# Sixty-four of 512 tokens leave the dense expert products and take gathered rows instead

## The chip, the core and the metric

The kernel runs on one core of a Trainium2 chip. A core has five engines that run their own instruction queues and meet at semaphores: PE (matrix products; its weight loads are listed apart as PEld), DVE (vector work), ACT (activations and copies), POOL (general work, and the queue of the software-made DMAs) and SP (which here only issues DMAs). SBUF is the on-chip memory of 128 partitions, PSUM the banks that PE writes. The metric is the device time of one execution in microseconds. The kernel before takes 2653.66 us, the median of three runs (2651.48 to 2654.41).

## The reference, cut to what matters

512 tokens of width 1024 go through two blocks. The first has a mixer (stick-breaking attention and a gated linear recurrence side by side) and then a PEER feed-forward; the second has a sliding-window layer and a sparse-attention layer. The change touches the mixer and the PEER part:

```python
def rg_lru(x, w_a, b_a, w_x, b_x, lam):       # x has been through a short causal convolution
    r = sigmoid(block_product(x, w_a) + b_a)
    i_gate = sigmoid(block_product(x, w_x) + b_x)
    log_a = -8.0 * r * softplus(-lam)
    b = sqrt(-expm1(2.0 * log_a)) * (i_gate * x)
    h_t = exp(log_a)_t * h_{t-1} + b_t        # a scan over the 512 tokens
o_rg = rg_lru(...) * gelu(g_rg)               # the gate multiplies what the scan gives

def peer_ffn(x, w_query, sub_keys, expert_u, expert_v):
    # 8 heads; each picks 16 of 16384 experts by two halves of a key
    idx, best_s = top16 of the sums of two top16 lists
    g = softmax(best_s)
    u = expert_u[idx]; v = expert_v[idx]      # one row of 1024 each
    act = gelu(x . u)
    return sum over the 128 picks of g * act * v
```

So a token needs 128 rows of U and 128 rows of V. All arithmetic is held to float32: a product is made of two rounded halves, hi and lo, and three matmuls (hi hi, hi lo, lo hi).

## The kernel before, in words

Activations lie transposed, features on the partitions and the 512 tokens along the row. Weights come as units of 512 KB. `Stream` loads a unit on SP's queue (`_dma`), rounds it to hi on ACT (`_hi`, line 145) and makes lo on DVE (`_lo`, line 154; on POOL for the units listed in `ON_POOL`). `gemm` (line 319) multiplies a unit: eight k-steps of three matmuls.

**The PEER part does not gather.** It computes the products of all 16384 experts with all tokens, in 128 chunks of 128 experts, and multiplies them by a dense matrix of gates that is zero for what a token did not pick. It has two stages:

- The s stage, 128 turns of `s_gemm` (line 937): 24 matmuls of 512 columns (lines 944 to 946), gelu on ACT, and a store to Sd in DRAM. Beside it runs the side work, `topk` (line 1047), as a Python generator whose steps `pace` mixes between the matmuls. A step yields its assumed cost on DVE and ACT, and `RATE` says how much of each fits into a chunk. Per tile of 128 tokens it finds the picks (`topk_tile`), and then in 32 steps of four tokens (`gate_tile`) builds the dense gates out of one-hot rows: comparisons on DVE, scaled copies on ACT, four or eight small products on PE, and stores to Gd in DRAM. The side work has to be over at chunk 122, where its memory is handed to the y stage.
- The y stage, 32 groups of four chunks. `w_part` (line 961) multiplies a chunk's s and gates (loaded back two chunks ahead by `prefetch` on POOL's queue) and splits the result: W on DVE, Wh on ACT, Wl on DVE. `y_part` (line 977) does 12 matmuls for one eighth of the features over the four chunks and adds them to the residual X on DVE. Each chunk of a group is followed by two `y_part`s.

**The mixer's order is written out by hand.** A projection takes eight slots, one per k-step. `put(i, f)` hangs a piece of other work on a slot, `take` hands the next eight to the unit that is being multiplied, and `self.at` is the first slot not yet taken. Every piece is thus issued behind a known matmul, on whatever engine it uses. The projections run: k and q of the first head pair, four g units (the gates, with the pieces of the bias table hung on them), four x units (each followed by convolution and two small gate products), four v units, and the next k and q. The recurrence's pieces (`rg_a` to `rg_e`, lines 638 to 655 and 527 to 535) hang on the slots after the x units, beside the v, k and q projections.

Of the kernel before, what the change touches and what calls it, by code (L numbers as in the profile page):

```python
# [42 lines left out]
TAIL = 6  # L43
WARM = 3

RATE = (4.6, 4.4)
# [67 lines left out]
ON_POOL = {"m": (1, 13, 15, 17, 26), "s": (2,), "n": (17,)}  # L114
# [93 lines left out]
class K:  # L208
# [267 lines left out]
    def mixer(self, dp, out_pool, bias):  # L476
# [50 lines left out]
        def rg_d(ct):  # L527
            s, u = xc[:, ct], it[:, ct]
            nc.vector.tensor_tensor_scan(s, rt[:, ct], u, 0.0, op0=MUL, op1=ADD)
            nc.gpsimd.tensor_tensor(u, gs[:, ct], s, op=MUL)  # L530

        def rg_e(ct):
            u = it[:, ct]
            square(ssr, u, ct == 0)
            self.gain_split(rgh[:, ct], rgl[:, ct], u, self.v("out_norm_rg", ct))


        with self.pool("maux", bufs=4, space=PSUM) as aux:
# [48 lines left out]
            def gelu(cs):  # L587
# [3 lines left out]
                nc.scalar.preload_act_table_set("sigmoid_and_others")  # L591
# [31 lines left out]

            for ct in range(4):
# [24 lines left out]
            def rg_c(ct):  # L649
                nc.vector.scalar_tensor_tensor(xc[:, ct], xc[:, ct], 2.0, y[ct], op0=MUL, op1=MUL)  # L650
                nc.gpsimd.tensor_tensor(it[:, ct], it[:, ct], xc[:, ct], op=MUL)
# [204 lines left out]
    def peer_pre(self, hraw, H):  # L856
# [5 lines left out]
        sgp = self.tc.alloc_tile_pool(name="sgp", bufs=2)  # L862
        tk = self.tc.alloc_tile_pool(name="tk", bufs=1)
        rscol = tk.tile([P, 4], F32, name="rscolf")
        top = lambda t: (tk.tile([P, 16, 16], F32, tag=f"tv{t % 2}", name="tv"),
                     tk.tile([P, 16, 16], U32, tag=f"ti{t % 2}", name="ti"), set())
        self.top = {t: top(t) for t in range(2)}
# [55 lines left out]
    def peer_main(self, sgp, tk, sc, rscol, H, Gd, Sd, pools, sums, fin):  # L923


        nc = self.nc
# [10 lines left out]
        def s_gemm(c, side=None):  # L937
            w = self.S.get(self.ui)
            self.ui += 1
            ps = sp.tile([P, T], F32, tag="s", name="s")  # L940
            hi, lo = w
            for k in range(KT):
                wh, wl = hi[:, k * P:(k + 1) * P], lo[:, k * P:(k + 1) * P]
                nc.tensor.matmul(ps, wh, h_hi[:, k], start=k == 0, stop=False)  # L944
                nc.tensor.matmul(ps, wh, h_lo[:, k], start=False, stop=False)  # L945
                nc.tensor.matmul(ps, wl, h_hi[:, k], start=False, stop=k == KT - 1)  # L946
# [4 lines left out]
        def prefetch(c):  # L951
            if c >= NCH:
                return
            g = pp.tile([P, T], F32, tag="G", name="G")
            nc.gpsimd.dma_start(g, Gd[c])  # L955
            s = pp.tile([P, T], F32, tag="sg", name="sg")
# [4 lines left out]
        def w_part(c):  # L961
# [7 lines left out]
            w = pp.tile([P, T], F32, tag="W", bufs=2, name="W")  # L969
            wh = pp.tile([P, T], F32R, tag="Wh", bufs=8, name="Wh")  # L970
            wl = pp.tile([P, T], F32R, tag="Wl", bufs=8, name="Wl")
# [5 lines left out]
        def y_part(gr, m):  # L977
            ps = yp.tile([P, T], F32, tag="y", name="y")
# [8 lines left out]
            nc.vector.tensor_tensor(self.X[:, m], self.X[:, m], ps, op=ADD)  # L987
            if gr == NG - 1:
                fin(m)

        side = self.topk(tk, gtp, gbp, ggp, trp, sc, rscol, Gd)
        cost = [0.0, 0.0]
        nside = NPRE - TAIL
# [13 lines left out]
        for c in range(NPRE):  # L1007
            if c == nside:
# [11 lines left out]
                yp = self.tc.alloc_tile_pool(name="pm_y", bufs=4, space=PSUM)  # L1020
            if c == NPRE - 5:
# [4 lines left out]
            ps = s_gemm(c, pace(c) if c < nside else None)  # L1026
            sg = sgp.tile([P, T], F32, tag="sg", name="sgo")
            nc.scalar.activation(sg, ps, AF.Gelu_apprx_tanh)  # L1028
            nc.gpsimd.dma_start(Sd[c], sg)  # L1029
            if c >= NPRE - 4:  # L1030
                w_part(c - (NPRE - 4))
        for gr in range(NG):
            self.S.vmax = 4 * (gr + 2)
            for j in range(4):
# [3 lines left out]
                y_part(gr, 2 * j + 1)  # L1038
# [1163 lines left out]
```

## Time and profile before

| | us |
|---|---|
| median of three runs | 2653.66 (2651.48 to 2654.41) |
| the profiled execution's own time | 2653.56 |
| its span, first to last instruction | 2651.7 |
| mixer | 0 to 262 |
| queries, scores and the start of top-k | 262 to 378.7 |
| s stage | 378.7 to 1188.7 |
| y stage | 1188.7 to 1909.5 |
| the two attention layers of the second block | 1909.5 to 2651.7 |

The ends of the stages are the first starts of the lines that belong to them. Over the span PE is busy 97%, DVE 69%, ACT 54% and POOL 16%. The granted TensorE clock is 0.991 of full speed. Matmuls are pipelined, so that the 0.4 us the profile gives for one of 512 columns is its length, and not the distance to the next one; distances are read from starts.

In the views below, a group's row has line, engine, operation, output and inputs by name, sizes and count, then the busy time in us and the mean length of one in ns, then the engine's idle time before it and what ended it. A timeline row has start and length in us. A row of waits has who waited for whom, the total in us, how often, and the longest. Where a matmul is in full float32 (not split into halves), the trace has two records for it.

### The profile page before, as it was taken

The page shows a single profiled execution, that of the slowest core. Times are in us where ns is not written, and L with a number is a line of the kernel's source. Part 1 is how long each engine was busy: PE and PEld are TensorE (multiplying, and loading weights), DVE is VectorE, ACT ScalarE, POOL GpSimd, SP SyncE. Part 2 cuts the span into 40 slices and gives each one's busy share as a digit, 9 for nine tenths or more (in the row PEclk, how much of TensorE's full clock was granted, in tenths as well). Part 3 has the DMA queues.
Part 4 walks back from the last instruction along what each step waited for, and adds up shares of the span by engine and source line. Part 5 has one row for each costly group of instructions (what it writes and reads, how often), then busy time and mean ns, then how long its engine had stood idle before and what let it go on. Part 6 is the DMA issues. An engine that isn't in the chain of part 4 may idle for free.

```text
span 2651.7 us, 33669 instructions
## 1 busy us (share of the span) xinstructions
PE 2584.7 (97%) x11920; PEld 2043.9 (77%) x11920; DVE 1829.8 (69%) x3674; ACT 1418.8 (54%) x2822; POOL 420.4 (16%) x615
## 2 busy tenths in 40 slices
PE   8889999999999999999999999999999989999998
PEld 5667778888888878788888888888777777777776
DVE  5787668777868869536666666666578634777774
ACT  5585434887787788532222222222377534656653
POOL 3313001011011100021111111111211120101011
PEclk9999999999999999999999999999999999999999
DMA  4221224377477676756555555555232252212113
GB/s 150 64 64 56 96 96 157 130 198 202 144 193 204 174 191 182 212 203 203 190 191 190 187 187 190 188 186 185 85 93 77 70 159 84 88 62 65 62 61 103
DMA packets 230936, 372.65 MB, mean 141 GB/s; under 512 B 147583, under 2 KB 147711, under 8 KB 230640
## 3 DMA queue, kind: packets, MB, share of 16 engines
q1 hardware_dynamic: 56016, 201.88, 22.9%
q0 software_dynamic: 40928, 131.74, 16.2%
q10 hardware_dynamic: 133824, 36.89, 6.4%
q8 instruction: 94, 1.54, 0.2%
q14 instruction: 74, 0.61, 0.1%
HBM read 293.76 MB, written 79.82 MB: 141 GB/s over the span
## 4 chain that ended last, share of the span: by engine, by line
PE 84%; DVE 8%; ACT 3%; issue 2%; DMA 1%; ACTq 1%; POOL 1%; SPq 0%; DVEq 0%; POOLq 0%
PE y L986 9%; PE y L985 9%; PE y L984 9%; PE s L944 9%; PE s L946 9%; PE s L945 9%; PE g L326 6%; PE g L328 6%; PE g L327 6%; PE gps L1214 2%; PE nO L1849 1%; PE gps L1207 1%; PE hp L1605 1%; PE nL L1792 1%; PE nT L1831 1%
## 5 line engine op out<-in xcount | busy, mean ns | idle before, releaser
L154 DVE TENSOR_TENSOR lo<-raw,hi 128x1024 fp32r<-128x1024 f32 x374 | 456.8, 1229 | 191.4 <-PE s L946 94.0
L145 ACT ACTIVATE hi<-raw 128x1024 fp32r<-128x1024 f32 x381 | 395.0, 1052 | 94.2 <-PE y L985 38.8
L944 PE MATMUL s<-h_hi,hi 128*128 128x512 f32 x1024 | 409.2, 400 | 3.8 <-ACT hi L145 2.3
L946 PE MATMUL s<-h_hi,lo 128*128 128x512 f32 x1024 | 406.6, 397 | 0.5 <-DVE lo L154 0.5
L986 PE MATMUL y<-Wh,lo 128*128 128x512 f32 x1024 | 405.9, 396 | 0.0
L985 PE MATMUL y<-Wl,hi 128*128 128x512 f32 x1024 | 405.9, 396 | 0.0
L984 PE MATMUL y<-Wh,hi 128*128 128x512 f32 x1024 | 405.9, 396 | 0.0
L945 PE MATMUL s<-h_lo,hi 128*128 128x512 f32 x1024 | 403.6, 394 | 0.0
L973 ACT ACTIVATE Wh<-W 128x512 fp32r<-128x512 f32 x128 | 80.9, 632 | 418.5 <-DVE W L972 418.5
L1195 ACT ACTIVATE ohg<-oh,gh 128x128 fp32r<-128x128 bf16 x960 | 292.6, 395 | 5.3 <-DVE oh L1177 5.3
L987 DVE TENSOR_TENSOR X<-X,y 128x512 f32<-128x512 f32 x256 | 175.1, 685 | 149.0 <-PE y L986 147.0
L946 PEld LDWEIGHTS s<-h_hi,lo 128*128 128x128 f32 x1024 | 192.9, 188 | 48.5 <-DVE lo L154 1.3
L985 PEld LDWEIGHTS y<-Wl,hi 128*128 128x128 f32 x1024 | 192.9, 188 | 47.1
L984 PEld LDWEIGHTS y<-Wh,hi 128*128 128x128 f32 x1024 | 192.9, 188 | 47.0
L986 PEld LDWEIGHTS y<-Wh,lo 128*128 128x128 f32 x1024 | 192.9, 188 | 47.0
L944 PEld LDWEIGHTS s<-h_hi,hi 128*128 128x128 f32 x1024 | 193.5, 189 | 43.6 <-ACT hi L145 2.7
L945 PEld LDWEIGHTS s<-h_lo,hi 128*128 128x128 f32 x1024 | 193.2, 189 | 41.7
L1029 POOL DMA_DIRECT2D Sd<-sgo x128 | 69.6, 544 | 820.2 <-ACT sgo L1028 820.2
L1028 ACT ACTIVATE sgo<-s 128x512 f32<-128x512 f32 x128 | 76.3, 596 | 219.3 <-issue 137.8
L1177 DVE TENSOR_TENSOR oh<-cst,sT 128x512 bf16<-128x512 f32 (+1 forms) x256 | 164.9, 685 | 24.7 <-ACT ohg L1195 24.1
L974 DVE TENSOR_TENSOR Wl<-W,Wh 128x512 fp32r<-128x512 f32 x128 | 88.6, 692 | 105.8 <-ACT Wh L973 105.8
L955 POOL DMA_DIRECT2D G<-Gd x128 | 68.7, 537 | 542.4 <-DVE W L972 542.2
(457 smaller groups left out, 4765.1 us busy)
## 6 DMA issues: line engine op xcount, KB each, us to landing
raw<-in_peer_u_dram SPq DMA_DIRECT2D x128, 512.0 KB, 3.8
raw<-in_peer_v_dram SPq DMA_DIRECT2D x128, 512.0 KB, 3.3
Sd<-sgo POOLq DMA_DIRECT2D x128, 256.0 KB, 3.2
Gd<-Gb ACTq DMA_DIRECT2D x64, 512.0 KB, 4.7
G<-Gd POOLq DMA_DIRECT2D x128, 256.0 KB, 4.1
sg<-Sd POOLq DMA_DIRECT2D x128, 256.0 KB, 4.2
raw<-in_b_w_in_dram SPq DMA_DIRECT2D x33, 512.0 KB, 3.2
raw<-in_w_in_dram SPq DMA_DIRECT2D x20, 512.0 KB, 3.3
```

Source lines behind the costliest of these rows:

```text
L145: self.k.nc.scalar.activation(hi, self.r[i], AF.Copy)
L154: eng.tensor_tensor(lo, raw, hi.bitcast(F32), op=SUB)
L326: nc.tensor.matmul(ps, wh, rh[:, k - k0], start=start and k == k0, stop=False)
L944: nc.tensor.matmul(ps, wh, h_hi[:, k], start=k == 0, stop=False)
L945: nc.tensor.matmul(ps, wh, h_lo[:, k], start=False, stop=False)
L946: nc.tensor.matmul(ps, wl, h_hi[:, k], start=False, stop=k == KT - 1)
L984: nc.tensor.matmul(ps, vh, wh, start=j == 0, stop=False)
L985: nc.tensor.matmul(ps, vh, wl, start=False, stop=False)
L986: nc.tensor.matmul(ps, vl, wh, start=False, stop=j == 3)
L987: nc.vector.tensor_tensor(self.X[:, m], self.X[:, m], ps, op=ADD)
L1177: nc.vector.tensor_tensor(o, iota[:, None, :].to_broadcast([P, 4, P]), sT[:, x, 4 * q:4 * q + 4][:, :, None].to_broadcast([P, 4, P]), op=EQ)
L1195: nc.scalar.activation(B[q][:, j, x], oh[:, j], AF.Copy, scale=gh[:, x, 4 * q + j:4 * q + j + 1])
```

## The change

The last 64 tokens (`NGT`) leave the dense scheme; `TD` = 448 remain. Five things are edited.

1. **Dense products.** In both stages the matmuls, the gelu, W, Wh, Wl, the X additions, and the Sd and Gd rows go over 448 columns.
2. **Gates.** `gate_tile` runs 16 of its 32 steps for the last token tile. Two instructions keep that tile's picks: `pick_i`, the expert's number, and `pick_g`, its gate, both with the 128 picks on the partitions and the 64 tokens along the row.
3. **Gathered rows.** A second generator, `gather`, runs beside the y stage. It first turns the 64 tokens' h back to tokens on partitions (16 small products, two copies). Per token it gathers 128 rows of U (512 KB) by an indirect DMA on POOL's queue, spreads the token's h over all partitions with a matmul against a repeated column of an identity, and on DVE multiplies and sums (`scalar_tensor_tensor` with `accum_out`, two halves of 512). After 64 tokens come gelu and gates, and then per pair of tokens four products of the gathered V rows with a 32-column weight that is zero but for one column, so that each token's result adds up in its own row of one PSUM bank, `acc`. The rows use the buffers that held the split U units (five of 512 KB), and are asked for three ahead. The generator is advanced after each chunk of the y stage, and once more in every second group.
4. **Pacing.** `RATE` goes from (4.6, 4.4) to (4.2, 4.0), and the memory is handed over as soon as the side work is done, if that is before chunk 122.
5. **Mixer.** The x units come before the g units. The g units now run behind the first three parts of the recurrence, and its scan and what follows hang on the slots after them. Four kinds of elementwise work of the recurrence and three lo splits go from POOL to DVE. The activation tables are reloaded in another order.

```diff
-RATE = (4.6, 4.4)
+NGT = 64
+TD = T - NGT
+RATE = (4.2, 4.0)
-ON_POOL = {"m": (1, 13, 15, 17, 26), "s": (2,), "n": (17,)}
+ON_POOL = {"m": (1, 26), "s": (2,), "n": (17,)}
...
         def rg_d(ct):
             s, u = xc[:, ct], it[:, ct]
             nc.vector.tensor_tensor_scan(s, rt[:, ct], u, 0.0, op0=MUL, op1=ADD)
-            nc.gpsimd.tensor_tensor(u, gs[:, ct], s, op=MUL)
+            nc.vector.tensor_tensor(u, gs[:, ct], s, op=MUL)
         def rg_e(ct):
-            square(ssr, u, ct == 0)
+            square(ssr, u, ct == 0, eng=nc.vector)
...
-            for ct in range(4):
-                self.peq = self.take()
-                ps = self.unit(gp, xh, xl)
-                self.put(self.at, gate_in, ct, ps)
-                if bias:
-                    self.put(self.at + 0, bias.pop(0))
-            self.put(self.at + 2, gelu, range(4))
...
-                    nc.gpsimd.tensor_tensor(it[:, ct], it[:, ct], xc[:, ct], op=MUL)
+                    nc.vector.tensor_tensor(it[:, ct], it[:, ct], xc[:, ct], op=MUL)
...
-                for j, g in ((3, rg_a), (6, rg_b), (9, rg_c), (10, rg_d), (16, rg_e)):
-                    self.put(i0 + 6 + 6 * ct + j, g, ct)
+                for j, g in ((3, rg_a), (6, rg_b), (9, rg_c)):
+                    self.put(i0 + 6 + 5 * ct + j, g, ct)
+            for ct in range(4):
+                self.peq = self.take()
+                ps = self.unit(gp, xh, xl)
+                self.put(self.at, gate_in, ct, ps)
+                if bias:
+                    self.put(self.at + 0, bias.pop(0))
+            self.put(self.at + 2, gelu, range(4))
+            for ct in range(4):
+                self.put(self.at + 7 + 4 * ct, rg_d, ct)
+                self.put(self.at + 20 + 8 * ct, rg_e, ct)
...
+                xh, xl = h_hi[:, k, 0:TD], h_lo[:, k, 0:TD]
+                nc.tensor.matmul(ps, wh, xh, start=k == 0, stop=False)
...
+        def gather():
+            hT = gq.tile([P, D], F32R, tag="hT", name="hT")
+            id2 = gq.tile([P, NGT], F32R, name="id2")
+            nc.vector.tensor_tensor(id2, ident[:, 0:NGT], ident[:, NGT:P], op=ADD)
+            for half in range(2):
+                ps = yp.tile([P, T], F32, tag="y", name="hTp")
+                for k in range(4):
+                    for x, hh in enumerate((h_hi, h_lo)):
+                        nc.tensor.matmul(ps[x * NGT:(x + 1) * NGT, k * P:(k + 1) * P],
+                                         hh[:, 4 * half + k, TD:].bitcast(F32), ident, start=k == 0,
+                                         stop=True, skip_group_check=True)
+                nc.scalar.activation(hT[:, half * T:(half + 1) * T], ps, AF.Copy)
+            order = [(0, t) for t in range(NGT)] + [(1, 32 * p + j) for j in range(32)
+                                                    for p in range(2)]
+            def fetch(i):
+                if i < len(order):
+                    x, t = order[i]
+                    x5 = i % 5 % 2
+                    rows[i] = wp.tile([P, D], F32, tag=("hi", "lo")[x5], bufs=3 - x5, name="row")
+                    nc.gpsimd.indirect_dma_start(
+                        rows[i], None, tables[x],
+                        bass.IndirectOffsetOnAxis(ap=idx[:, t:t + 1], axis=0))
+            yield
+            for i in range(3):
+                fetch(i)
+            yield
+            for t in range(NGT):
+                r = rows.pop(t)
+                for half in range(2):
+                    o = slice(half * T, (half + 1) * T)
+                    bc = sp.tile([P, T], F32, tag="s", name="hrow")
+                    nc.tensor.matmul(bc, id2[:, t:t + 1].to_broadcast([P, P]), hT[:, o],
+                                     start=True, stop=True)
+                    nc.vector.scalar_tensor_tensor(r[:, o], r[:, o], 1.0, bc, op0=MUL, op1=MUL,
+                                                   accum_out=dots[:, half, t:t + 1])
+                fetch(t + 3)
+                yield
+            w = gq.tile([P, NGT], F32, name="gw")
+            nc.vector.tensor_tensor(w, dots[:, 0], dots[:, 1], op=ADD)
+            nc.scalar.activation(w, w, AF.Gelu_apprx_tanh)
+            nc.vector.tensor_tensor(w, w, gate, op=MUL)
+            acc = yap.tile([P, T], F32, name="yacc")
+            for j in range(32):
+                yield
+                r = [rows.pop(NGT + 2 * j + p) for p in range(2)]
+                wx = gq.tile([P, 2, 32], F32, tag="wx", bufs=3, name="wx")
+                for p in range(2):
+                    nc.vector.tensor_scalar(wx[:, p], iota[:, 0:32], float(j),
+                                            w[:, 32 * p + j:32 * p + j + 1], op0=EQ, op1=MUL)
+                for half in range(2):
+                    for p in range(2):
+                        q = 32 * (2 * p + half)
+                        nc.tensor.matmul(acc[q:q + 32, :], wx[:, p],
+                                         r[p][:, half * T:(half + 1) * T], start=j == 0,
+                                         stop=j == 31, skip_group_check=True)
+                fetch(NGT + 2 * j + 3)
+                fetch(NGT + 2 * j + 4)
+                yield
...
+            if c == NPRE - 2:
+                next(rest)
         for gr in range(NG):
+            if gr == NG - 2:
+                for _ in rest:
+                    pass
+            if gr % 2 == 1:
+                next(rest, None)
             for j in range(4):
                 if gr + 1 < NG:
                     w_part(4 * (gr + 1) + j)
                 y_part(gr, 2 * j)
                 y_part(gr, 2 * j + 1)
+                next(rest, None)
...
+        nq = 16 if tt == 3 else 32
-        for q in range(35):
+        for q in range(nq + 3):
...
-        first = [("k", 0), ("q", 0)] + [(t, i) for t in "gxv" for i in range(4)] + [("k", 1), ("q", 1)]
+        first = [("k", 0), ("q", 0)] + [(t, i) for t in "xgv" for i in range(4)] + [("k", 1), ("q", 1)]
```

At the end of `gather`, `acc` is copied, turned by four transposes and added to the last 64 tokens of X in two instructions. The rows of U come from a second copy of the table that lies by expert (`peer_ur`); V already does.

More of the change, by code (lines that the diff above doesn't have):

```diff
@@ L866, in peer_pre @@
                      tk.tile([P, 16, 16], U32, tag=f"ti{t % 2}", name="ti"), set())
+        self.picked = (tk0.tile([P, NGT], U32, name="pick_i"), tk0.tile([P, NGT], F32, name="pick_g"))
         self.top = {t: top(t) for t in range(2)}
@@ L939, in s_gemm @@
             self.ui += 1
-            ps = sp.tile([P, T], F32, tag="s", name="s")
+            ps = sp.tile([P, T], F32, tag="s", name="s")[:, 0:TD]
             hi, lo = w
@@ L977, in y_part @@
         def y_part(gr, m):
-            ps = yp.tile([P, T], F32, tag="y", name="y")
+            ps = yp.tile([P, T], F32, tag="y", name="y")[:, 0:TD]
             for j in range(4):
@@ L986, in y_part @@
                 nc.tensor.matmul(ps, vl, wh, start=False, stop=j == 3)
-            nc.vector.tensor_tensor(self.X[:, m], self.X[:, m], ps, op=ADD)
+            nc.vector.tensor_tensor(self.X[:, m, 0:TD], self.X[:, m, 0:TD], ps, op=ADD)
             if gr == NG - 1:
                 fin(m)
+        tables = A["peer_ur"], A["peer_v"].rearrange("c p d -> (c p) d")
+        idx, gate = self.picked
+        wp = pools["w"]
+        def gather():
+            ident, iota = self.c("ident"), self.c("iota")
+            hT = gq.tile([P, D], F32R, tag="hT", name="hT")
[9 more added lines that the diff above has]
+                nc.scalar.activation(hT[:, half * T:(half + 1) * T], ps, AF.Copy)
+            dots = gq.tile([P, 2, NGT], F32, name="dots")
+            order = [(0, t) for t in range(NGT)] + [(1, 32 * p + j) for j in range(32)
+                                                    for p in range(2)]
+            rows = {}
+            def fetch(i):
[42 more added lines that the diff above has]
+                yield
+            yT = gq.tile([P, D], F32, tag="hT", name="yT")[:, 0:T]
+            nc.scalar.activation(yT, acc, AF.Copy)
+            ps = sp.tile([P, T], F32, tag="s", name="yTp")
+            for b in range(4):
+                nc.tensor.transpose(ps[:, b * P:(b + 1) * P], yT[:, b * P:(b + 1) * P], ident)
+            pv = ps.rearrange("c (b p h t) -> c b p h t", b=4, p=2, h=2)
+            for half in range(2):
+                o = self.X[:, 4 * half:4 * half + 4, TD:].rearrange("c b (p t) -> c b p t", p=2)
+                nc.vector.tensor_tensor(o, o, pv[:, :, :, half], op=ADD)
@@ L1007, in peer_main @@
         for c in range(NPRE):
-            if c == nside:
+            if not done and (c == nside or cost[0] >= 1e9):
+                done = True
                 for d in side:
@@ L1020, in peer_main @@
                 yp = self.tc.alloc_tile_pool(name="pm_y", bufs=4, space=PSUM)
+                yap = self.tc.alloc_tile_pool(name="pm_ya", bufs=1, space=PSUM)
+                gq = self.tc.alloc_tile_pool(name="gq", bufs=1, side="right")
+                rest = gather()
             if c == NPRE - 5:
@@ L1025, in peer_main @@
                 self.bias_rows.pop(0)()
-            ps = s_gemm(c, pace(c) if c < nside else None)
-            sg = sgp.tile([P, T], F32, tag="sg", name="sgo")
+            ps = s_gemm(c, None if done else pace(c))
+            sg = sgp.tile([P, TD], F32, tag="sg", name="sgo")
             nc.scalar.activation(sg, ps, AF.Gelu_apprx_tanh)
@@ L2090, in run @@
         if "p" in stages:
[L2091 to L2092 removed]
+            Gd = dp.tile([P, P, TD], F32, name="Gd")
+            Sd = dp.tile([NPRE, P, TD], F32, name="Sd")
             after = next((then[x] for x in "sn" if x in stages), None)
```

43 lines of the change are left out of this document (26 added, 17 removed).

## The prediction

> **What bounds the kernel now.** I read the busy time by stage first.
>
> ```profile
> 0.00:130.00 130.00, 115.87 (x438) 81.68 (x438) 85.98 (x112) 66.99 (x95) 42.05 (x50) 0.96 0.33 109
> 130.00:262.00 132.00, 119.29 (x600) 92.15 (x600) 109.75 (x143) 94.60 (x156) 37.45 (x26) 0.96 0.18 56
> 378.70:1188.70 810.00, 805.09 (x3788) 660.86 (x3789) 592.22 (x1304) 575.70 (x1369) 91.27 (x169) 1.00 0.63 181
> 1188.70:1909.50 720.80, 720.07 (x3074) 578.57 (x3072) 474.39 (x637) 214.41 (x266) 139.14 (x253) 1.00 0.56 182
> 1909.50:2651.70 742.20, 710.57 (x3482) 537.46 (x3482) 491.95 (x1244) 422.09 (x868) 103.00 (x114) 0.99 0.27 84
> ```
>
> Columns: length, then PE, PEld, DVE, ACT and POOL busy, granted clock, DMA share, GB/s. The third and fourth rows are the two dense expert stages (s: U products with top-k and gates beside them; y: V products). PE is busy 99% and 100% there, so their 1531 us are a count of matmuls times a pitch. The last row is not touched. The first two, the mixer, have PE idle for 27 us.
>
> The pitch, from the places of one line's 1024 executions and from a stretch of shorter matmuls:
>
> ```profile
> L984 PE MATMUL y<-Wh,hi x1024: 391/397/400, 1188.9 to 1907.9; 128*128 128x512 f32 x171
> ```
> ```profile
> 206.14 0.40 PE L732 MATMUL z<-sl,cr 128*128 128x512 f32 x1
> 206.38 0.34 PE L732 MATMUL z<-sh,cr 128*128 128x384 f32 x1
> 206.55 0.34 PE L732 MATMUL z<-sl,cr 128*128 128x384 f32 x1
> 206.73 0.28 PE L732 MATMUL z<-sh,cr 128*128 128x256 f32 x1
> ```
>
> The y loop issues three matmuls per turn: 719.0 / (3 x 1023) = 0.2343 us for 512 columns. 384 columns take (206.73 - 206.38) / 2 = 0.175, which is 0.75 x 0.2343: the pitch follows the columns, and loading weights sets no floor at this width. So 448 columns take 0.2050.
>
> **The change part by part.** *Fewer columns.* 3072 matmuls in each of s and y lose 0.0293 us: 90.0 us in each stage.
>
> *Fewer gates.* For the last token tile, 16 of 32 gate steps go, each with four products:
>
> ```profile
> 1001.49 1.29 DVE L1177 TENSOR_TENSOR oh<-cst,sT 128x512 bf16<-128x512 f32 x2
> 1002.84 0.63 PE L1207 MATMUL gps<-ohg,oh 128*128 128x256 f32 x4
> 1003.31 0.40 PE L944 MATMUL s<-h_hi,hi 128*128 128x512 f32 x1
> ```
>
> They hold PE 1003.31 - 1002.84 = 0.47 us per step: 16 x 0.47 = 7.5 us. The two new selection instructions hide under DVE's slack. Eight stores to Gd go as well.
>
> *What could eat it in s.* The side work must fit a shorter chunk.
>
> ```profile
> 980.00:1094.00 114.00, 113.80 (x543) 93.80 (x544) 100.05 (x140) 97.49 (x254) 9.17 (x17) 0.99 0.70 189
> sum 566.00, PE 565.39 PEld 467.04 DVE 453.74 ACT 455.99 POOL 59.96; mean PE 141.35 PEld 116.76 DVE 113.44 ACT 114.00 POOL 14.99
> ```
>
> Over four windows of this stage (566 us; the row is the busiest) DVE and ACT are at 80%. Their share of the 3072 matmuls is about 566 / 810, so PE loses 2147 x 0.0293 = 63 us there; with the same side work that would make 90%. The pacing constants fall by 9%, which spreads it over more chunks: about 85%. Loss between 0 and 12 us (the busiest window, where DVE's 100.05 meets 114 less 12.5); I take 4. s: 810 - 90 - 7.5 + 4 = 716.5, a gain of 93.5.
>
> *y, U rows of 64 tokens.* 128 broadcast matmuls of 512 columns on PE: 128 x 0.2343 = 30.0 us. 64 gathers on POOL's queue. On DVE, two 512-wide multiply-and-sum per token. Rows of DVE in y:
>
> ```profile
> L987 DVE TENSOR_TENSOR X<-X,y 128x512 f32<-128x512 f32 x256 | 175.1, 685 | 149.0 <-PE y L986 147.0
> L154 DVE TENSOR_TENSOR lo<-raw,hi 128x1024 fp32r<-128x1024 f32 x125 | 149.7, 1218 | 0.3 <-ACT hi L145 0.3
> L974 DVE TENSOR_TENSOR Wl<-W,Wh 128x512 fp32r<-128x512 f32 x125 | 86.5, 692 | 97.8 <-ACT Wh L973 97.8
> L972 DVE TENSOR_TENSOR W<-sg,G 128x512 f32<-128x512 f32 x124 | 84.8, 684 | 0.0
> L849 DVE SCALAR_TENSOR_TENSOR h_lo<-X,vec,h_hi 128x512 fp32r<-128x512 f32 x7 | 5.2, 745 | 0.0
> ```
>
> The helper advances 4.5 times per group of four chunks, so a chunk carries 1.125 tokens for about 57 chunks. PE per chunk: 24 x 0.2050 + 2.25 x 0.2343 = 5.45 us. DVE, laid end to end: 1.22 (lo) + 4 x 0.60 (448 columns) + 2.25 x 0.745 (the nearest row to the new instruction) + 0.75 waiting for ACT's Wh = 6.05. But neighbours overlap: two of 0.685 took 1.29 above, 0.08 less each, 0.58 for 7.25 instructions: 5.47. A tie. If it slips, Wl and the X addition are late behind it, and PE waits for a y buffer. Between 0 and 0.60 x 57 = 34 us; nearer the tie, because the overlap is measured, and I take 10 for the whole stage.
>
> *y, V rows.* Per pair of tokens four fp32 products of 32 output columns and 512 moving ones, in four column groups. The trace has such products in pairs (64 + 64) and alone:
>
> ```profile
> 200.69 0.40 PE L328 MATMUL p<-gr,lo 128*128 128x512 f32 x1
> 201.02 1.72 PE L746 MATMUL o<-w,V 128*64 128x512 f32 x8
> 202.67 0.50 PE L326 MATMUL p<-gr,hi 128*128 128x512 f32 x1
> 203.01 0.39 PE L327 MATMUL p<-rr,hi 128*128 128x512 f32 x1
> ```
> ```profile
> 2309.03 1.12 PE L1905 MATMUL cO<-cPT,nVC 64*128 64x512 f32 x2
> 2310.08 0.50 PE L326 MATMUL g<-bh,hi 128*128 128x512 f32 x1
> ```
>
> Alone: 1.05 us for 512 columns, 2.05 ns per column. In pairs: 1.65 us for 2 x (512 + 384), 0.92: two ran at once. Entering and leaving cost 0.10 and 0.11. Nothing here shows four at once. Bounds per token pair (2048 columns): 0.94 + 0.2 if four run at once, 1.88 + 0.2 if two, 4.2 + 0.2 if none; over 32 pairs 36.5, 67 or 141 us. I take 36.5, since halving the width already halved the time. The Trainium skill ("TensorE: Matmul & The Clock Gate", Part 3, measured speedup) gives 2.38 for three 32-column products at once; stretched to about 3.1 for four, an estimate, it makes 1.55 us per pair and 50 us, 13 more than my sum. Turning the 64 tokens' rows for the broadcast and the result back: 16 products of 128 columns at 0.92 ns and four alone, 3 us.
>
> y: 720.8 - 90 + 30.0 + 36.5 + 3 + 10 = 710.3, a gain of 10.5. That gain is small: the gathered half costs on PE nearly what the columns save.
>
> *Transfers.* 128 gathers of 512 KB are added to y, beside 67 MB of V and 59 MB of Gd and Sd rows.
>
> ```profile
> q1 hardware_dynamic: 56016, 201.88, 22.9%
> q0 software_dynamic: 40928, 131.74, 16.2%
> ```
> ```profile
> L955 POOL DMA_DIRECT2D G<-Gd x128 | 68.7, 537 | 542.4 <-DVE W L972 542.2 <-issue 0.3
> L154 POOL TENSOR_TENSOR lo<-raw,hi 128x1024 fp32r<-128x1024 f32 x7 | 18.0, 2573 | 16.4 <-PE g L328 8.8 <-ACT hn_y L307 6.9 <-ACT hi L145 0.7
> ```
>
> By share of 2651.7 us, q1 needs 3.01 us per MB over all engines, q0 3.26. y then: 67 x 3.01 + (59 + 67) x 3.26 = 612 us of 710, 86% instead of 56%. The rows are asked for three tokens ahead, some 14 us, so I count them as hidden; without that cover a row late by t stops DVE (U half) or PE itself (V half, where the product waits at the head of PE's queue and the y matmuls stand behind it). No row shows an indirect issue: from 0.54 us (a plain one) to 2.57 (POOL's longest row), per chunk at most 2 x 0.54 + 1.125 x 2.57 = 4.0 of 5.45. G and sg queue behind the gathers on POOL, two chunks early, and SP's V loads keep their own queue. I take the issue as hidden. Two other new waits are on PE: each broadcast needs one of three s banks, which DVE frees, and the first V product needs the gated weights, made one step earlier. ACT gets four short copies and one gelu; it is busy 214 of 720.80 us.
>
> *Mixer.*
>
> ```profile
> PE g L326 <- DVE hn_m L405: 4.5, 2, 4.2
> PE g L328 <- DVE lo L154: 3.8, 2, 3.2
> PE bvp L1279 <- DMA oh<-in_onehot_dram: 3.6, 1, 3.6
> PE vtp L438 <- DVE vt L433: 2.7, 1, 2.7
> ```
> ```profile
> 115.00:140.00 25.00, 14.86 (x57) 10.53 (x56) 24.79 (x22) 10.46 (x17) 16.20 (x10) 0.83 0.17 60
> L530 POOL TENSOR_TENSOR i<-g,x 128x512 f32<-128x512 f32 x4 | 6.7, 1680 | 7.7 <-DVE x L529 7.7
> L647 DVE SCALAR_TENSOR_TENSOR rgy<-rgt,rgy 128x512 f32<-128x512 f32 x4 | 6.8, 1692 | 0.1
> L650 DVE SCALAR_TENSOR_TENSOR x<-x,rgy 128x512 f32<-128x512 f32 x4 | 2.8, 689 | 0.1
> ```
>
> Between 30 and 140 us PE waits 14.6 us. At 115 to 140 DVE is full: the same kind of instruction takes 1.69 us on L647 and 0.69 on L650, next to POOL's additions. Afterwards four g units (96 matmuls, 22 us) lie over the recurrence, the bias pieces run in them, 22 us later than the transfer they waited 3.6 us for, and 15 POOL instructions and three lo splits become DVE's: 15 x 0.69 + 3 x 1.22 = 14 us more, against at least 4 us of slowdown gone. ACT reloads a table once more; it is busy 67 of 130 us. SP issues the same loads with x before g. Between -14.6 (all waits go) and +4 (the 14 us stay, 10 of the waits go); I take -10.
>
> **Sum.** 2651.7 - 93.5 - 10.5 - 10 = 2537.7, plus 1.9 outside the span (2653.56 - 2651.7): 2540 us. The profiled run is 0.1 below the median, so nothing is corrected.
>
> **Rivals.**
> *Two column groups at a time.* +30.5: 2570. For: the pairs showed two and no more. Against: nothing in them that stops at two. None at once: +104, 2644.
> *DVE or a late row sets the first half of y.* Laid end to end, +34 less the 10 allowed, 2564; were the V half held as long by transfers at 86%, 2598. I price it between, at 2580. For: the tie. Against: the measured overlap.
> *POOL's gather issue sets y, and the kernel gets slower.* If an indirect issue costs x, POOL needs 128x + 256 x 0.537 = 128x + 137 us. It binds from x = 4.5; from x = 5.4 (y at 823) nothing is gained. At three times POOL's longest row, 7.7, y is 1123: 2953. For: no row has one. Against: a plain issue over 128 partitions is 0.54. The Trainium skill ("GPSIMD Engine Reference", section 7) speaks against this change: about 102 cycles per small read command, such as one per gather index, not overlapped. With 128 indices at its 1.2 GHz that is 10.9 us, an estimate, and y about 1530; no run here shows it.
> *The columns save nothing* (a floor under 0.234): both 90s are gone, 2540 + 180 = 2720. The 384-column rows speak against it.
>
> **How the numbers follow.** Forecast 0.57 (own range 2521 to 2568: all mixer waits gone and no allowances, or +4 in the mixer and both allowances doubled); two groups 0.15; late rows 0.12; none at once 0.03; POOL 0.06; no saving 0.02; unforeseen 0.05, of which faster 0.01, no change 0.02 and slower 0.02. About 0.2% is what a measurement here can tell. Faster 0.88, within it 0.02, slower 0.10. The range 2512 to 2600 takes in the first three cases, 0.84, less some of their edges.
>
> **What would show it.** Pitch of the s and y matmuls 0.205; s 717 us long, y 710; the four V products of a pair starting together; PE without waits for bc or y buffers; POOL's gather row under 4 us; PE's waits of 30 to 140 gone. Wrong if y is longer than before, if a gather row exceeds 5.4 us, or if s stays above 740.

## The result and the profile after

The changed kernel takes 2565.62 us (median of 4 executions, 2564.78 to 2566.72), the kernel before beside it 2654.03 (2651.48 to 2656.0): a ratio of 0.9668, 95% interval 0.9651 to 0.9684, 88 us faster. The forecast was 2540. The profiled execution of the changed kernel has a span of 2563.3 us where the sum of the prediction had 2537.7; the excess of 25.6 is what the rest of this document accounts for.

Busy time by stage of the changed kernel: length, then PE, PEld, DVE, ACT and POOL busy, granted clock, DMA share, GB/s. The y stage is cut at the last broadcast's product and at the last V product.

```profile
0.00:130.00 130.00, 115.72 (x426) 81.05 (x427) 93.77 (x134) 72.17 (x102) 21.11 (x37) 0.93 0.34 109
130.00:256.00 126.00, 119.53 (x614) 92.82 (x612) 100.75 (x139) 90.83 (x151) 27.03 (x20) 1.00 0.19 59
256.00:372.60 116.60, 113.90 (x541) 93.22 (x541) 75.36 (x239) 44.88 (x70) 7.37 (x5) 0.97 0.28 94
372.60:1091.10 718.50, 713.36 (x3755) 653.02 (x3756) 547.83 (x1243) 531.69 (x1259) 91.18 (x169) 1.00 0.66 192
1091.10:1411.90 320.80, 315.31 (x1535) 287.23 (x1535) 275.24 (x549) 93.16 (x120) 137.46 (x188) 1.00 0.87 294
1411.90:1760.00 348.10, 319.10 (x1616) 261.51 (x1616) 208.96 (x355) 90.40 (x116) 129.30 (x177) 1.00 0.75 254
1760.00:1822.20 62.20, 62.20 (x314) 58.12 (x312) 39.74 (x59) 23.43 (x32) 12.00 (x17) 1.00 0.37 122
1822.20:2563.30 741.10, 709.90 (x3483) 536.52 (x3482) 491.48 (x1245) 422.06 (x868) 104.08 (x115) 0.99 0.27 84
```

| stretch | before | predicted | after |
|---|---|---|---|
| ahead of s | 378.7 | 368.7 | 372.6 |
| s | 810.0 | 716.5 | 718.5 |
| y | 720.8 | 710.3 | 731.1 |
| behind y | 742.2 | 742.2 | 741.1 |

20.8 of the 25.6 us lie in y. It is even longer than before the change (731.1 against 720.8), which the prediction had named as a sign of being wrong: the 88 us come from s (91.5) and the mixer (6.1), and in y the change loses 10.3.

The sixth row of the profile is the one to stop at: in the V half PE is idle for 29 of 348 us, while PE is busy 98% in the U half and all the time once the gathered work is over. PE's waits in the two halves (waiting line, what it waited for, us in total, times, longest):

```profile
PE hrow L1043 <- DVE row L1045: 5.5, 7, 1.7
```
```profile
PE yacc L1066 <- DVE wx L1061: 22.9, 25, 1.3
PE yacc L1066 <- DMA G<-Gd: 6.1, 7, 0.9
```

The products of V (L1066) wait for `wx`, the one-hot weights that DVE makes. The rows around one pair show how (start, length, engine and line, what it computes, idle time before it):

```profile
1504.52 0.36 PE L996 MATMUL y<-Wh,lo 128*128 128x448 f32 x1
1504.92 0.62 DVE L997 TENSOR_TENSOR X<-X,y 128x448 f32<-128x448 f32 x1 [0.64 <-PE y L996]
1505.46 0.38 DVE L1061 TENSOR_SCALAR wx<-cst,gw 128x32 f32<-128x32 f32 x2
1505.75 0.30 PEld L1066 LDWEIGHTS yacc<-row,wx 128*32 128x32 f32 x8 [1.23 <-DVE wx L1061]
1505.75 1.21 PE L1066 MATMUL yacc<-row,wx 128*32 128x512 f32 x8 [0.87 <-DVE wx L1061]
...
1506.88 0.47 PE L994 MATMUL y<-Wh,hi 128*128 128x448 f32 x1
```

The last y matmul ends, DVE adds the finished sum to X (0.62), then makes the two sets of weights (0.38 for both), and only when the first is there can PE's next instruction start: 1.23 us after the matmul before it, in all 32 pairs (smallest distance 1.222, median 1.226, mean 1.266), where the next y matmul would have followed after 0.20. A pair's four products leave eight records, two each; they start in two groups of four (in the pairs looked at 0.00, 0.15, 0.15, 0.16 and 0.45, 0.60, 0.61, 0.61 us after the first), and the next y matmul follows 1.13 us after the first. So four do run beside one another. The 0.15 is a wait too: the two weight instructions end 0.146 apart.

The stall was open to three readings when the trace alone was there; the first experiment's expectation has them under the same numbers. Theory 1: it is this chain on DVE. Theory 2: going over to four column groups costs PE about 1 us, whatever DVE does; the constancy speaks for it. Theory 3: rows and transfers are late, with the transfer engines at 0.75 to 0.87 and seven of the waits put down to a transfer.

### The profile page after: what moved, and what is told of

Its sections match the earlier page's. It is cut to its first block, busy times and chain, and to the rows that moved or that the text cites. A ratio compares the mean times of both kernels' runs of the same rounds, so it can differ in the third digit from the quotient of the medians.

```text
span 2563.3 us, 34776 instructions
## 1 busy us (share of the span) xinstructions
PE 2469.0 (96%) x12276; PEld 2063.5 (81%) x12276; DVE 1833.1 (72%) x3955; ACT 1368.6 (53%) x2715; POOL 529.5 (21%) x725
## 4 chain that ended last, share of the span: by engine, by line
PE 61%; DVE 11%; issue 4%; ACT 3%; DMA 2%; ACTq 1%; POOL 0%; DVEq 0%; POOLq 0%
PE s L954 7%; PE s L956 7%; PE s L955 7%; PE y L994 6%; PE y L996 6%; PE y L995 6%; PE g L328 4%; PE g L330 4%; PE g L329 4%; DVE lo L156 2%; PE gps L1327 2%; PE nO L1962 2%; PE yacc L1066 1%; PE hp L1718 1%; DVE row L1045 1%
## 5 line engine op out<-in xcount | busy, mean ns | idle before, releaser
L954 PE MATMUL s<-h_hi,hi 128*128 128x448 f32 x1024 | 379.4, 370 | 3.9 <-ACT hi L147 2.4
L956 PE MATMUL s<-h_hi,lo 128*128 128x448 f32 x1024 | 376.3, 367 | 0.6 <-DVE lo L156 0.6
L955 PE MATMUL s<-h_lo,hi 128*128 128x448 f32 x1024 | 376.3, 368 | 0.0
L994 PE MATMUL y<-Wh,hi 128*128 128x448 f32 x1024 | 376.1, 367 | 0.0
L995 PE MATMUL y<-Wl,hi 128*128 128x448 f32 x1024 | 372.7, 364 | 0.0
L996 PE MATMUL y<-Wh,lo 128*128 128x448 f32 x1024 | 372.1, 363 | 0.0
L983 ACT ACTIVATE Wh<-W 128x448 fp32r<-128x448 f32 x128 | 74.0, 578 | 422.7 <-DVE W L982 415.8
L997 DVE TENSOR_TENSOR X<-X,y 128x448 f32<-128x448 f32 x256 | 153.2, 616 | 116.0 <-PE y L996 115.6
L996 PEld LDWEIGHTS y<-Wh,lo 128*128 128x128 f32 x1024 | 192.1, 188 | 14.6
L1290 DVE TENSOR_TENSOR oh<-cst,sT 128x512 fp32r<-128x512 f32 (+1 forms) x224 | 144.3, 685 | 20.1 <-ACT ohg L1308 20.1
L984 DVE TENSOR_TENSOR Wl<-W,Wh 128x448 fp32r<-128x448 f32 x128 | 80.0, 625 | 98.8 <-ACT Wh L983 98.8
```

The lines of the kernel that those rows point to most:

```text
L954: nc.tensor.matmul(ps, wh, xh, start=k == 0, stop=False)
L955: nc.tensor.matmul(ps, wh, xl, start=False, stop=False)
L956: nc.tensor.matmul(ps, wl, xh, start=False, stop=k == KT - 1)
L994: nc.tensor.matmul(ps, vh, wh, start=j == 0, stop=False)
L995: nc.tensor.matmul(ps, vh, wl, start=False, stop=False)
L996: nc.tensor.matmul(ps, vl, wh, start=False, stop=j == 3)
```

## The experiments

Each time is a median; the ratio is to the kernel before, run beside it on the same chip (2652.03 us, and 2654.09 beside the last two of the U half). Differences between two experiments of 2 to 3 us are within their spread.

**Weights one step earlier.** The same two DVE instructions, ahead of the chunk's y matmuls instead of behind the addition:

```diff
             for j in range(32):
-                yield
-                r = [rows.pop(NGT + 2 * j + p) for p in range(2)]
                 wx = gq.tile([P, 2, 32], F32, tag="wx", bufs=3, name="wx")
                 for p in range(2):
                     nc.vector.tensor_scalar(wx[:, p], iota[:, 0:32], float(j),
                                             w[:, 32 * p + j:32 * p + j + 1], op0=EQ, op1=MUL)
+                yield
+                r = [rows.pop(NGT + 2 * j + p) for p in range(2)]
```

> The one-hot weights of a V pair (two DVE instructions) are issued one step earlier, ahead of the chunk's y matmuls instead of behind the addition that waits for the last of them; nothing else moves. After the change a pair starts 1.23 us (median) after the last y matmul instead of 0.20. Theory 1 (the weights' DVE chain, end of the y matmuls, addition 0.62, weights 0.38, is what PE waits for): the gap falls to 0.2 to 0.3 us, 32 x 1.0 = 31 to 34 us less, total 2532 to 2536, V half near 316. Theory 2 (PE itself needs about 1 us to go over to four column groups): the gap stays at 1.2, total 2565. Theory 3 (the gathered rows are late, the weights only finish near them): the gap stays partly, and its waits name the rows; 2545 to 2565.

Measured: 2534.3 us (2531.05 to 2536.3), ratio to before 0.9556 (0.954 to 0.9572). A pair of this kernel in time, and its y stage by windows:

```profile
1507.89 0.36 PE L996 MATMUL y<-Wh,lo 128*128 128x448 f32 x1
1508.18 1.06 PE L1066 MATMUL yacc<-row,wx 128*32 128x512 f32 x8
1508.29 0.62 DVE L997 TENSOR_TENSOR X<-X,y 128x448 f32<-128x448 f32 x1 [1.46 <-PE y L996]
1508.83 0.38 DVE L1059 TENSOR_SCALAR wx<-cst,gw 128x32 f32<-128x32 f32 x2
...
1509.18 0.47 PE L994 MATMUL y<-Wh,hi 128*128 128x448 f32 x1
```
```profile
1089.30:1411.90 322.60, 316.77 (x1533) 287.86 (x1532) 275.19 (x547) 93.28 (x120) 136.08 (x188) 0.99 0.87 291
1411.90:1725.40 313.50, 310.90 (x1617) 258.19 (x1616) 208.29 (x354) 89.31 (x115) 129.84 (x175) 1.00 0.82 282
1725.40:1787.90 62.50, 62.50 (x315) 58.41 (x314) 40.35 (x59) 24.40 (x34) 13.24 (x19) 1.00 0.39 124
```

The product now starts 0.29 us after the last y matmul (median and smallest; mean 0.38), while the addition and the next pair's weights lie beside it on DVE. The V half is 313.5 us instead of 348.1, y 698.6 instead of 731.1. Theory 1 holds, and theory 2 is left with 0.09 us a pair. The waits put down to a transfer are gone as well, though the rows are asked for at the same place as before. Moving two instructions beats both kernels by more than the error.

**All V products in one column group.**

```diff
+            nc.vector.memset(acc, 0.0)
...
-                        q = 32 * (2 * p + half)
-                        nc.tensor.matmul(acc[q:q + 32, :], wx[:, p],
-                                         r[p][:, half * T:(half + 1) * T], start=j == 0,
+                        nc.tensor.matmul(acc[0:32, :], wx[:, p],
+                                         r[p][:, half * T:(half + 1) * T],
+                                         start=j + half + p == 0,
```

> The changed kernel with all four V products of a pair in the first column group and one accumulator, so that none can run beside another; the number of products and their sizes stay. The result of the last 64 tokens is given up (four sums are mixed). Theory 1 (the four groups run at once, as the records' starts 7 ns apart show): four times 0.94 instead of one per pair, 32 x 2.8 = 90 us more, 2650 to 2660. Theory 2 (the starts are only the record's, the products run one behind another anyway): within 5 us of 2566. Theory 3 (two at once): +30 to +35, 2596 to 2601.

Measured: 2644.21 us (2639.24 to 2648.24), ratio 0.9969 (0.9957 to 0.998): 79 us above the changed kernel. That is theory 1, 6 us below its range: a product takes 0.89 us instead of 0.94, and the four together take 1.13 in the changed kernel. One pair, and the V half:

```profile
1432.04 3.62 PE L1066 MATMUL yacc<-row,wx 128*32 128x512 f32 x8 [0.87 <-DVE wx L1062]
1435.59 0.48 PE L994 MATMUL y<-Wh,hi 128*128 128x448 f32 x1
```
```profile
1413.00:1840.00 427.00, 397.68 (x1631) 280.69 (x1630) 211.27 (x358) 90.48 (x116) 125.22 (x177) 1.00 0.64 209
```

The distance before the first product is unchanged (median 1.226), which speaks once more against the reading that going over to four groups costs PE the time: there are none here to go over to. From the first product to the next y matmul it is 3.55 us against 1.13, or 1.00 with the early weights, where the second product does not wait for its weights: four column groups are worth a factor of 3.1 as the changed kernel has them and 3.6 without that wait. Of the 88 us that the change gained, 79 hang on them. The edit also lets the four add up in the same rows of the bank; the y matmuls do that as well and start 0.200 us apart, but no run here takes the two apart.

**No rows fetched** (after the first five). On top of the early weights:

```diff
-                if i < len(order):
+                if 5 <= i < len(order):
+                    rows[i] = rows0[i % 5]
+                elif i < len(order):
...
+                    rows0[i] = rows[i]
...
-                    nc.vector.scalar_tensor_tensor(r[:, o], r[:, o], 1.0, bc, op0=MUL, op1=MUL,
+                    nc.vector.scalar_tensor_tensor(r[:, o], r[:, o], 0.05, bc, op0=MUL, op1=MUL,
```

> The kernel with early weights (2534 us), with rows fetched for the first five steps only; the later steps reuse these five buffers, so 123 of 128 gathers (64 MB) are left out and the last 64 tokens' result is given up (the factor 1.0 of the dot products becomes 0.05, so that reused rows do not grow). All work of PE, DVE and ACT stays. Theory 1 (rows and their transfers are hidden behind the dense products): within 4 us of 2534. Theory 2 (transfers at 0.87 of their engines slow the dense units or the rows): 10 us or more less, 2524 or lower.

Measured: 2536.31 us (2529.64 to 2542.63), ratio 0.9558 (0.9533 to 0.9582). The four executions spread over 13 us, so the halves of y say more than the total:

```profile
1093.00:1416.00 323.00, 316.76 (x1525) 286.36 (x1524) 273.82 (x543) 93.26 (x120) 71.33 (x126) 0.99 0.57 189
1416.00:1731.00 315.00, 312.40 (x1624) 259.45 (x1623) 209.62 (x358) 89.51 (x115) 60.67 (x115) 1.00 0.55 181
```

The DMA share of the U half falls from 0.87 to 0.57, POOL's busy time by half, and neither half gets shorter (322.6 and 313.5 with the early weights alone). The transfers are hidden.

**Dense products only.** The changed kernel with nothing in place of the gathered half:

```diff
-                rest = gather()
+                rest = iter(())
...
-                next(rest)
+                next(rest, None)
```

> The changed kernel without the gathered half: 448 dense columns, the last 64 tokens get no expert sum at all (left out). By the y matmuls' 0.200 us in the changed kernel, 3072 of them are 614 us and y is 616 to 620 instead of 731.1, total 2451 to 2455. By the predicted 0.205, 630 + 3, total 2468. If the gathered half cost PE only its own instructions (30 + 36 us, with no waits about them), y would be 731.1 - 66 = 665 and the total 2500: that is the rival to the reading that 34 us of waits for the weights and some 9 us of waits in the U half belong to it.

Measured: 2446.79 us (2445.55 to 2447.65), ratio 0.9227 (0.9212 to 0.9242). Its y stage:

```profile
1088.20:1702.70 614.50, 614.50 (x3074) 576.54 (x3072) 435.75 (x635) 208.26 (x266) 138.00 (x253) 1.00 0.62 201
```
```profile
L994 PE MATMUL y<-Wh,hi x1024: 362/362/372, 1088.3 to 1702.1; 128*128 128x448 f32 x171
```

PE never idles, and 613.8 / (3 x 1023) = 0.2000 us per matmul. The total lies 4 us under the expected 2451 to 2455. In y the gathered half therefore costs 731.1 - 614.5 = 116.6 us in the changed kernel and 698.6 - 614.5 = 84.1 with early weights. Put together from the starts of PE's records (us, the distance from each matmul to the next, summed by kind):

| y stage | changed | early weights | one column group |
|---|---|---|---|
| y matmuls (distances to anything but a product) | 616.4 | 616.2 | 618.1 |
| 128 broadcasts, with their waits | 37.1 | 37.4 | 37.2 |
| last y matmul to the first product, 32 | 40.5 | 12.1 | 40.8 |
| first product to the next y matmul, 32 | 36.3 | 32.3 | 113.6 |

The columns add up to within 1 us of the three y stages (731.1, 698.6 and 810.1).

**The U half.** What is left there is the wait for a free s bank. Three runs, all on top of the early weights, ask whether it or DVE sets that half. DVE is busy 275 of its 323 us; the 288 in the expectation of the second run is the number beside it, PE's weight loads. PE's wait for the bank in the kernel with early weights:

```profile
PE hrow L1043 <- DVE row L1045: 5.8, 7, 2.1
```

First the extra step of every second group, put into the middle of the group, so that four broadcasts do not meet:

```diff
-            if gr % 2 == 1:
-                next(rest, None)
             for j in range(4):
...
                 y_part(gr, 2 * j)
+                if gr % 2 == 1 and j == 2:
+                    next(rest, None)
```

> The kernel with early weights (2534 us), with the extra step of every second group moved from right behind another step into the middle of the group. At the old place four broadcasts follow one another with three s banks, and the PE waits for DVE to free one (7 times, 5.8 us on the matmuls; the 71 distances between two broadcasts have a mean of 0.33 instead of 0.23, 7 us in all). Theory 1 (the bank wait comes from the two steps meeting): 6 to 8 us less, 2526 to 2528. Theory 2 (DVE is full in the U half, the wait goes elsewhere): within 2 us of 2534.

Measured: 2532.13 us (2530.34 to 2535.26), ratio 0.9549 (0.9533 to 0.9565). PE's waits for the bank become longer at the new place:

```profile
PE hrow L1043 <- DVE row L1045: 9.3, 8, 1.6
```

Theory 2: no difference from 2534 that can be told, and the bank is late for another reason than the two steps' meeting. Next, dot products over half the columns:

```diff
+                    o = slice(half * T, half * T + T // 2)
-                    nc.vector.scalar_tensor_tensor(r[:, o], r[:, o], 1.0, bc, op0=MUL, op1=MUL,
+                    nc.vector.scalar_tensor_tensor(r[:, o], r[:, o], 1.0, bc[:, 0:T // 2], op0=MUL, op1=MUL,
```

> The kernel with early weights (2534 us), each of the 128 dot products in the U half taken over 256 columns instead of 512 (half of the dot product is left out, so the last 64 tokens' result is given up); PE, transfers and the rest stay. DVE is busy 288 of the U half's 323 us. Theory 1 (DVE is the engine that is full there): its work falls by some 34 us, PE's waits for a free s bank go, the U half becomes 313 to 316 us, total 2525 to 2528. Theory 2 (something else on PE or among the transfers sets the U half): within 2 us of 2534.

Measured: 2533.01 us (2531.26 to 2538.43), ratio 0.9542 (0.9526 to 0.9557). The U half, the V half, and two waits in the U half:

```profile
1092.20:1412.00 319.80, 317.07 (x1541) 288.15 (x1540) 245.49 (x551) 95.14 (x121) 138.88 (x190) 1.00 0.85 295
1412.00:1730.00 318.00, 315.40 (x1606) 255.21 (x1604) 205.51 (x350) 88.65 (x113) 127.04 (x173) 1.00 0.80 276
```
```profile
PE hrow L1043 <- DVE row L1046: 2.7, 7, 0.6
DVE X L997 <- PE y L996: 28.1, 31, 1.7
```

DVE loses 30 us of work and PE 3 us of waits. The rest of what DVE was spared turns into waiting for PE: 28.1 us ahead of the X addition, where it was 3.1 with the early weights alone. The half takes 319.8 us; with the full dot products it took 322.6 in that run and 320.8 in the changed kernel, so a gain in length cannot be told from the spread. Theory 1 falls at the size I gave it: DVE is not what sets the U half. PE is. In the kernel with early weights 1403 y matmuls at 0.200 (280.6) and 128 broadcasts at 0.2343 (30.0) fill 311 of its 322.6 us; the waits at the broadcasts take 7 more, and 5 are y matmuls above 0.200, 1.6 of them in one stretch of 3.4 us at half the clock (granted 0.50). Last, the product of gates and gelu on POOL:

```diff
-            nc.vector.tensor_tensor(w, s, g, op=MUL)
+            (nc.gpsimd if 4 <= c < 60 else nc.vector).tensor_tensor(w, s, g, op=MUL)
```

> The kernel with early weights (2534 us), the product of gates and gelu of 56 chunks (all of the U half) on POOL instead of DVE; nothing is left out. DVE has 56 x 0.62 = 35 us less, POOL 56 x 1.5 = 84 more beside its 136 of 323. Theory 1 (DVE is full and POOL is free beside it): the U half 313 to 316 us, total 2525 to 2528. Theory 2 (as in the mixer before the change, where DVE took 1.69 instead of 0.69 us next to POOL's additions: DVE slows by what it is spared): 2532 to 2550.

Measured: 2535.44 us (2532.14 to 2543.72), ratio 0.9563 (0.9545 to 0.9581): nothing gained. Groups of this kernel's U half (busy us, mean ns):

```profile
L1031 POOL DMA_INDIRECT row<-in_peer_ur_dram,pick_i x64 | 97.6, 1524 | 62.0 <-DVE row L1045 56.7 <-issue 4.7 <-DVE Wl L984 0.3
L156 DVE TENSOR_TENSOR lo<-raw,hi 128x1024 fp32r<-128x1024 f32 x60 | 90.4, 1528 | 0.3 <-ACT hi L147 0.3
...
L982 POOL TENSOR_TENSOR W<-sg,G 128x448 f32<-128x448 f32 x56 | 71.3, 1273 | 0.3
```

The splits on DVE take 1.53 us instead of 1.22, 18 us more over 60, which is half of the 35 us that DVE was spared; with PE the bound, neither counts for much.

**The mixer part alone**, on the kernel before; the diff is the mixer's hunks of the change and nothing of the experts (all 512 tokens dense).

> The kernel before with the recurrence part of the change alone: input gates projected behind the recurrence's gates, the small POOL products on DVE; experts as before (512 dense tokens). The prediction gave this part -10 us (between -14.6 and +4); in the changed kernel the stretch ahead of the s stage ended 6.1 us earlier. Theory 1 (the part is worth what that boundary showed): 2648. Theory 2 (it is worth the predicted 10 and the experts' part gives 4 back before the s stage): 2644. Theory 3 (it is worth nothing by itself): 2654.

Measured: 2647.48 us (2646.18 to 2648.8, 10 executions) against 2652.03, ratio 0.9981 (0.9972 to 0.9991): 5 us, with an interval of 2 to 7. Theory 1. PE's waits ahead of the s stage in this kernel:

```profile
PE g L327 <- DVE xl L294: 4.3, 3, 1.8
PE gate L597 <- DVE x L613: 4.1, 1, 4.1
...
PE g L328 <- DVE lo L154: 1.5, 2, 1.1
...
PE g L326 <- DVE hn_m L405: 0.3, 1, 0.3
```

The waits of before for the bias pieces (3.6), for `hn_m` (4.5) and most of that for `lo` (3.8) are gone. In the changed kernel the four waits of PE between 25 and 140 us come to 8.2 us, where those of before were 14.6: 6.4 less, which is the 6.1 of the boundary. New is one of 4.1 us for `x`, the first convolution (L613, L615 in the changed kernel). Its place in the changed kernel, on PE and DVE:

```profile
37.45 0.39 PE L330 MATMUL g<-xh,lo 128*128 128x512 f32 x1
37.60 0.69 DVE L417 TENSOR_TENSOR hn_x<-hn_x,hn_a 128x512 f32<-128x512 f32 x1
...
39.52 2.32 DVE L615 SCALAR_TENSOR_TENSOR x<-xp,vec,x 128x512 f32<-128x512 f32 x3
41.90 1.22 PE L599 MATMUL gate<-x,wbd 128*128 128x512 f32 x1 [4.06 <-DVE x L615]
```

Four g units no longer stand ahead of it, so the convolution comes right behind other work of DVE (L417), and the gate matmuls stand five slots behind it while it takes DVE until 41.8. To see whether that one can be had back, on top of the early weights:

```diff
-                self.spread((lambda: mm(0), lambda: mm(1), post), (5, 5, 7))
+                self.spread((lambda: mm(0), lambda: mm(1), post), (11, 11, 13) if ct == 0 else (5, 5, 7))
```

> The kernel with early weights (2534 us), with the first pair of gate matmuls of the recurrence put six slots later among the projection's matmuls, behind the first convolution, for which PE waits 4.1 us (the largest new wait of the changed mixer). Theory 1 (that wait is what the mixer part fell short by): 4 us less, 2530. Theory 2 (the chain of the recurrence behind the gates is as late as that, and a later wait takes its place): within 2 us of 2534.

Measured: 2531.03 us (2529.47 to 2541.78), ratio 0.9557 (0.9535 to 0.9579), not told apart from 2534. The wait for `x` is gone from the list, and another stands at its head (the s stage starts at 370.6 us instead of 371.3):

```profile
PE g L330 <- DVE lo L156: 5.2, 3, 3.6
PE g L329 <- DVE xl L296: 4.0, 4, 1.7
```

L330's wait for `lo` was 1.5 us before this edit and is 5.2 after it: most of the 4.1 us came back as a wait for DVE's next split (3.6 us at 43.5, behind the convolution). The trace bears out theory 2; the time alone, 3 us less, would not tell the two apart.

## Why the prediction was right, and where it was wrong

The direction, the s stage and most of the mechanism held; the forecast was 26 us too low, inside its range. For y not even the direction held: forecast 10.5 us shorter, it became 10.3 longer.

*Pitch.* Predicted 0.2050 for 448 columns. In s it is 0.205 (median of the starts), in y 0.200 (mean 0.203). Scaling by columns was right in s and a little cautious in y: the y matmuls take 622.8 us of the changed kernel, counting one pitch of 0.2 for each of the 32 ahead of a product, where the forecast had 630.8, and the dense stage alone 614.5.

*s stage.* Predicted 716.5, measured 718.5. By the distances of the starts its products lost 88.7 us (forecast 90), and the gate products 4.7 (forecast 7.5); turning the 64 tokens' h took 1.9 here and not in y. The 4 us allowed for the side work do not show: PE is idle 5.1 us where it was 4.9.

*V products.* Predicted 1.14 us per pair with 0.2 for entering and leaving, 36.5 in all. With early weights a pair costs (12.1 - 32 x 0.2 + 32.3) / 32 = 1.19. The lower bound was the right choice, and the rivals of two groups (2570) and none (2644) fall: with one group the kernel measures 2644.21. That the rival's price of 2644 agrees is partly chance, since its base of 2540 was 26 too low and its cost of 104 was 25 too high. The time alone would have chosen wrongly: 2565.62 lies nearer to the two groups' 2570 than to the forecast. It takes the starts of the products and the run with one group to rule two groups out.

*The step that failed* is one sentence of the part on transfers: "the first V product needs the gated weights, made one step earlier". It named the right wait and priced it at nothing on a misreading of the code. What is made once and early is `gw`, all 64 tokens' gated activations. What the product takes is `wx`, made from it by two DVE instructions directly ahead of the four products and behind the `yield`, so they stand in DVE's queue behind the addition of the y part just issued, and that addition waits for PE's last y matmul. PE then waits for DVE, which waits for PE: 40.5 - 32 x 0.2 = 34 us of distance where 0.1 a pair was counted. The prices of its links were in the trace of before (the addition on DVE is the same instruction); the order was in the diff. The early weights put this at 31 us of the total.

*What was luck.* V products and their wait cost 70.4 us on PE (40.5 - 32 x 0.2 + 36.3) instead of 36.5, 33.9 too much, and the broadcasts 7.1 too much. Against that the pitch gave back 8.0, and the 10 us allowed and the 3 for turning rows covered an error for which they were not meant. Without these 21 us the time would have been near 2587, beyond the forecast's own range to 2568.

*Allowances in y.* 10 us were kept for a near tie of DVE and PE in the U half. The tie is there: DVE is busy 275.2 of that half's 320.8 us and waits another 45.9 for ACT's `Wh`. What it cost PE is the 7.1 us at the broadcasts (37.1 instead of 30.0), for the reason named, a free s bank: with half the dot products they took 34.3, with the extra step put apart 41.1. DVE itself is not the bound: 30 us less of its work took 3 us of PE's waits. The rival in which DVE or a late row sets the first half falls, although its price (2564 to 2598) begins at the measured time: it would have put the loss in the U half, and it lies in the V half.

*Transfers.* Predicted 86% of the transfer engines in y; it was 0.77 over all of y, 0.87 in the U half and 0.75 in the V half, and leaving 64 MB out gave nothing. POOL's gather row of the U half in the changed kernel (the V half's has a median of 1.006):

```profile
L1031 POOL DMA_INDIRECT row<-in_peer_ur_dram,pick_i x64: 1001/1011/1866, 1095.4 to 1388.8; - x64
...
DMA to landing us min/median/max: 4.3/5.4/9.1
```

1.01 us per issue, between the bounds of 0.54 and 2.57 and far from the 5.4 at which nothing would have been gained. That rival (2953) falls, and with it the reading of the Trainium skill's "GPSIMD Engine Reference", section 7, by which 102 cycles per index made 10.9 us, an estimate: the measured issue is a tenth of it, so that rule, which stands there for Q7 kernels, does not describe this gather.

*Mixer.* Predicted -10, measured -6.1 at the boundary and 5 alone. The mechanism was right in the main (the recurrence's waits go when the input gates cover it), but the prediction's sign, PE's waits of 30 to 140 gone, did not come: 8.2 of 14.6 us are left. Half of that is the new wait for `x`, where with the input gates moved away the first convolution meets DVE's work of the start; the run with the later gate matmuls shows that it is not simply to be had back. Its price was within the range given (-14.6 to +4).

The sum of the differences: y +20.8, mixer +3.9, s +2.0, the rest -1.1, together 25.6.

## What to carry to other kernels

When new work is put between the steps of a loop that is bound by one engine, follow each operand of its first instruction back to the queue it is made in and ask what stands ahead of it there: here instructions of 0.2 us on an engine that was busy 60% of the half cost PE 1 us a time, because they queued behind one that waited for PE itself. Make such operands one step before they are needed: moving two lines gained 31 us. An engine that has no slack beside the bound is not yet the cause. Take work away from it in one run, and see whether it then waits for the bound.

## What the runs showed of the hardware that was not expected

In y the 448-column matmuls start 0.200 us apart where 0.8750 of the 0.2343 of before is 0.2050; in s they keep 0.205. Within one kernel the pitch changes for tens of microseconds between 0.200 and 0.207 at a granted clock of 1.00 in the row: in the V half of the run with halved dot products it is 0.207 for most of the time and that half takes 318.0 us, against 313.5 with the same work at 0.200. This is of the size of the differences between the last runs, and its cause stays open. At a granted clock of 0.50 the same matmuls start 0.373 us apart (3.4 us of the U half of the run with early weights).

Four products of 32 output columns and 512 moving ones take 1.00 us together (1.13 where the second waits for its weights) and 3.55 one behind another. The Trainium skill ("TensorE: Matmul & The Clock Gate", Part 3) has 2.38 for three; the prediction's stretch to 3.1 for four, an estimate, lies below the 3.6 measured where nothing waits.

An indirect fetch of 128 rows of 4 KB occupies POOL for 1.01 us, twice a plain one (0.54 in the trace of before), and for 1.52 (mean) in the run where POOL also multiplies.
